# Identity transposes in the waits of the matmul engine, tied behind the last dense matmul

## The chip, the cores and the metric

The kernel runs on one core of a Trainium2 chip. The metric is the time of one execution of the whole program on the device, in microseconds (us), lower is better. The engines are TensorE (PE: matmuls, and transposes done as matmuls against an identity matrix), VectorE (DVE), ScalarE (ACT), GpSimd (POOL) and SyncE (SP), whose queue issues most weight loads.

## The reference

256 tokens of width 1024 go through one block of one architecture and then two layers of another, all in float32.

```python
def reference(x, ...):
    x = first_block(x, p, ...)     # retention + sliding-window attention, merged, w_out;
                                   # then a mixture of 32 experts (top 2), then a gated embedding
    return second_block(x, c_2, ctx_2, ...)

def second_block(x, c, ctx, ...):
    for i in range(DEPTH_2):       # 2 layers, over x and over a context of the same form
        mod = (s_c @ w_mod[i] + b_mod[i])[:, None, :]
        ...
        h = modulate(rms_norm_2(x, g_norm1[i]), sh1, sc1)
        p = h @ w_in[i]
        ...                        # neighbourhood attention, spatial gating, latent attention
        x_new = x + gt1 * mix
        x_new = x_new + gt2 * squared_relu_mlp(modulate(rms_norm_2(x_new, g_norm2[i]), sh2, sc2),
                                               ffn_w1[i], ffn_w2[i])
```

The change touches no value that reaches the output.

## The kernel before

Every weight is streamed from HBM once, in pieces of 128x1024 float32. Each dense product is done as three matmuls on split operands: ACT rounds a piece to its high part `wh` (L187), DVE subtracts to get the low part `wl` (L188), and PE accumulates high by high, high by low and low by high. `dense_b` (L268 to L270) keeps the activation stationary and streams up to 512 columns; `mm_a` (L245 to L247) keeps the weight stationary and streams the 256 tokens.

Between two dense products of the main path stands a norm: ACT sums the squares (L291, L299), DVE does a Newton iteration for the inverse root (`newton`, L178 to L183), ACT and DVE scale the rows (L321, L322), PE transposes them by 128x128 (`turn`, L332), DVE and ACT evacuate the result with gain and shift (L343) and split it (L187, L188). Only then can the next dense product begin.

Work that is off this path is run beside it: the context's layer beside the router and the experts of block 1 (`moe`), the modulation matrices (`w_mod`, L709, L720), the context's keys. A scheduler of the framework orders the instructions of each engine from the order and the priorities in which the program was traced, so a stage's place in the queue of an engine is set when the program is built; on the chip each engine then takes its queue strictly in order.

PSUM has four pairs of banks, `pd`, `cd` (dense results) and `ps`, `cs` (small results, such as transposes), taken in turn. Of the stages named below: `dense_b` in block 1's output projection (writes `pd`); `router`, whose transposes are L767 and whose products are L772; `experts`, whose gathered rows are transposed at L925 and multiplied by the expert weights at L935 (the weights lie in slots `ew`, loaded by SP as slots come free), beside the context's latent keys (L1472 to L1489, transposed in `heads_T`, L1444); `gm_mix`, whose transposes are L1581 and products L1592; and `ffn`, which calls `turn`. L1317 transposes queries, L1080 multiplies queries and keys.

Of the kernel before, what the change touches and what calls it, by code (L numbers as in the profile page):

```python
# [163 lines left out]
class Build:  # L164
    def __init__(self, nc, tc, ins, out, dbg=None):
        self.nc, self.tc, self.i, self.out, self.dbg = nc, tc, ins, out, dbg or {}
        self.sides = []
        self.made = 0
        self.W2, self.wturn = None, 0
        self.flip = 0  # L170
        self.sturn = 0

    def newton(self, st, ss, n, scale, eps=EPS, eng=None):
# [65 lines left out]
    def mm_a(self, ps, x, w, f):  # L239
        mm = self.nc.tensor.matmul  # L240
        xh, xl = x
        n = len(w)
        s = slice(f * 128, f * 128 + 128)
        for k, (wh, wl) in enumerate(w):
            mm(ps, wh[:, s], xh[:, k], start=k == 0, stop=False)  # L245
            mm(ps, wh[:, s], xl[:, k], start=False, stop=False)  # L246
            mm(ps, wl[:, s], xh[:, k], start=False, stop=k == n - 1)  # L247

# [7 lines left out]

    def dense_b(self, st, x, view, put, width=512):
        mm = self.nc.tensor.matmul
        xh, xl = x
        K = view.shape[1]  # L260
        for c in range(0, view.shape[2], width):
            ps = [st.dense()[:, :width] for _ in range(2)]
            for k0, w in self.pieces(st, view[:, :, c:c + width]):
                for t in range(2):
                    s = slice(t * 128, t * 128 + 128)
                    for j, (wh, wl) in enumerate(w):
                        k = k0 + j
                        mm(ps[t], xh[:, k, s], wh, start=k == 0, stop=False)  # L268
                        mm(ps[t], xh[:, k, s], wl, start=False, stop=False)  # L269
                        mm(ps[t], xl[:, k, s], wh, start=False, stop=k == K - 1)  # L270
            for t in range(2):
                put(t, c, ps[t])

    def evac(self, dst, src):
# [49 lines left out]

    def turn(self, st, xn, gain=None, mod=None, out=None):
        nc = self.nc
        h, l = out or self.hl(st, 8)
        for j in range(4):
            ps = st.small_ps().rearrange("p (k t) -> p k t", k=2)
            for kk in range(2):  # L330
                for t in range(2):
                    nc.tensor.transpose(ps[:, kk, t * 128:t * 128 + 128], xn[t][:, 2 * j + kk], self.ident)  # L332
            if mod is None:
                for kk in range(2):
                    k = 2 * j + kk
                    g = gain[:, k:k + 1]
                    nc.scalar.activation(h[:, k], ps[:, kk], AF.Copy, scale=g)
                    nc.vector.scalar_tensor_tensor(l[:, k], ps[:, kk], g, h[:, k].bitcast(F32), op0=ALU.mult, op1=ALU.subtract)
            else:
                src = st.a(2).rearrange("p (k t) -> p k t", k=2)  # L340
                for kk in range(2):
                    k = 2 * j + kk
                    nc.vector.tensor_scalar(src[:, kk], ps[:, kk], mod[0][:, k:k + 1], mod[1][:, k:k + 1],  # L343
                                            op0=ALU.mult, op1=ALU.add)
                self.split(h[:, 2 * j:2 * j + 2], l[:, 2 * j:2 * j + 2], src)
        return h, l
# [10 lines left out]
    def run_all(self):  # L357
        nc, tc, i = self.nc, self.tc, self.i
        with ExitStack() as ctx:
# [61 lines left out]
            x0.rows(st)  # L421
            x0.turn(st)
            x0.start()
# [229 lines left out]
    def block1_out(self, st, mh):  # L653
        nc, i = self.nc, self.i

        def put_out(t, c, ps):
            xs = self.x[:, t, c:c + 512]
            nc.vector.tensor_tensor(xs, ps, xs, op=ALU.add)

        self.dense_b(st, mh, kp(i["w_out"][0], 8), put_out)  # L660

# [68 lines left out]
    def router(self, st, act):  # L730
# [32 lines left out]
        for j in range(4):  # L763
            ps = st.small_ps().rearrange("p (k t) -> p k t", k=2)
            for kk in range(2):
# [140 lines left out]
    def experts(self, st):  # L906
# [11 lines left out]
        for g in range(8):  # L918
            he = hes.pop()
            heT = st.a(4, tag="heT", bufs=1).rearrange("p (k s) -> p k s", k=8)  # L920
            for j in range(2):
                ps = st.small_ps().rearrange("p (k s) -> p k s", k=4)
                for kk in range(4):
                    c = (4 * j + kk) * 128
                    nc.tensor.transpose(ps[:, kk], he[:, c:c + 128], self.ident)  # L925
                self.evac(heT[:, 4 * j:4 * j + 4], ps)
            if g < 7:
                hes.append(gather(g + 1))
            pg = st.small_ps()
            for u in range(2):  # L930
                for kh in range(2):
# [221 lines left out]
class Layer:  # L1153
# [84 lines left out]

    def turn(self, st):
        self.xT = self.b.turn(st, self.xn, mod=(self.A[:, 0], self.mc[:, 0]), out=self.b.xT_tiles())  # L1240

# [318 lines left out]
    def gm_mix(self):  # L1560
# [26 lines left out]
        for j in range(2):  # L1587
            ps = st.small_ps().rearrange("p (g n q) -> p g n q", g=2, n=2)
            for gg in range(2):
# [41 lines left out]
    def ffn(self, meanwhile=None):  # L1631
# [3 lines left out]
        if meanwhile:  # L1635
            meanwhile()
        xT = b.turn(st, xn, mod=(self.A[:, 1], self.mc[:, 3]))
        w1 = pk(i["ffn_w1_2"][l], 8)
# [49 lines left out]
```

## Time and profile before

| what | value |
|---|---|
| median of 3 runs | 1928.05 us (1917.57, 1928.05, 1931.88) |
| the profiled execution | 1929.36 us, span 1926.9 us |
| PE | 1795.2 us busy, 93% of the span, 12572 matmuls |
| DVE, ACT, POOL | 1245.0 us (65%), 906.9 us (47%), 215.4 us (11%) |
| mean granted clock of PE | 0.976 |
| HBM | 232 GB/s over the span |

The profile is of one execution. "Idle before" is the time an engine stood still ahead of an instruction, and what follows the arrow is the instruction whose end released it. The granted clock is the share of full speed that PE was given: 1.0 is 2.4 GHz and 0.5 is 1.2 GHz.

### The profile page before, as it was taken

To read this page: it belongs to the slowest core of one execution; us is meant where nothing else is said; L and a number is where in the kernel's file an instruction comes from. 1 tells how busy PE (TensorE), PEld (TensorE's weight loads), DVE (VectorE), ACT (ScalarE), POOL (GpSimd) and SP (SyncE) were. 2 spreads that over 40 slices of the span, in tenths; PEclk is the share of its full clock that TensorE was granted. 3 is DMA by queue.
4 is the path that set the end of the run, shared out by engine and by line. 5 is a ranking of instruction groups with operands and counts; after the bars stand their busy time and mean duration, and the time that the engine had idled before them with its cause. 6 is when DMAs were issued, how large, how long until landed. Compare 5 with 4: busy or idle time off the path is not lost. (4 is left out here: it accounts for less than half of the span.)

```text
span 1926.9 us, 32425 instructions
## 1 busy us (share of the span) xinstructions
PE 1795.2 (93%) x12572; PEld 1474.3 (77%) x12572; DVE 1245.0 (65%) x2377; ACT 906.9 (47%) x1395; POOL 215.4 (11%) x209
## 2 busy tenths in 40 slices
PE   5999877999999999979899989999999899998998
PEld 3677856677786777765676878799998888787998
DVE  3554566664566545454768597866678887866665
ACT  3433434473444433334534465544456555554443
POOL 3000110100110101110121010011100210010110
PEclk9999988999999999989999999999999999998999
DMA  9788856889999998977787752555667655254652
GB/s 283 240 314 281 270 158 223 283 292 335 346 330 373 312 356 320 350 271 265 239 252 211 225 192 88 175 165 187 196 186 235 182 133 164 77 197 132 196 190 95
DMA packets 277172, 448.82 MB, mean 233 GB/s; under 512 B 35582, under 2 KB 182380, under 8 KB 276568
## 3 DMA queue, kind: packets, MB, share of 16 engines
q1 hardware_dynamic: 266344, 417.30, 65.0%
q0 software_dynamic: 10672, 29.43, 5.2%
q8 instruction: 99, 1.62, 0.3%
q14 instruction: 57, 0.47, 0.1%
HBM read 430.77 MB, written 15.86 MB: 232 GB/s over the span
## 5 line engine op out<-in xcount | busy, mean ns | idle before, releaser
L188 DVE TENSOR_TENSOR wl<-raw,wh 128x1024 fp32r<-128x1024 f32 (+2 forms) x484 | 610.3, 1265 | 366.5 <-ACT wh L187 207.3
L187 ACT ACTIVATE wh<-raw 128x1024 fp32r<-128x1024 f32 (+2 forms) x484 | 504.6, 1045 | 571.9 <-PE pd L246 117.6
L247 PE MATMUL pd<-xT,wl 128*128 128x256 f32 x384 | 108.9, 283 | 5.6 <-DVE wl L188 5.6
L245 PE MATMUL pd<-xT,wh 128*128 128x256 f32 x384 | 108.5, 283 | 0.4 <-DVE b_a L279 0.4
L246 PE MATMUL pd<-xT,wh 128*128 128x256 f32 x384 | 108.9, 283 | 0.0
L245 PE MATMUL cd<-b_a,wh 128*128 128x256 f32 x328 | 92.2, 281 | 0.0
L246 PE MATMUL cd<-b_a,wh 128*128 128x256 f32 x328 | 92.1, 281 | 0.0
L247 PE MATMUL cd<-b_a,wl 128*128 128x256 f32 x328 | 91.6, 279 | 0.0
L935 PE MATMUL ps<-ew,m_heT 128*32 128x256 f32 x1024 | 76.3, 386 | 8.2 <-DMA ew<-in_w_exp_up_dram 6.8
L247 PE MATMUL pd<-e_a,wl 128*128 128x256 f32 x288 | 82.3, 286 | 0.4 <-DVE wl L188 0.4
L245 PE MATMUL pd<-e_a,wh 128*128 128x256 f32 x288 | 82.4, 286 | 0.0
L246 PE MATMUL pd<-e_a,wh 128*128 128x256 f32 x288 | 81.8, 284 | 0.0
L246 PE MATMUL cd<-xT,wh 128*128 128x256 f32 x288 | 81.6, 283 | 0.0
L247 PE MATMUL cd<-xT,wl 128*128 128x256 f32 x288 | 81.3, 282 | 0.1
L245 PE MATMUL cd<-xT,wh 128*128 128x256 f32 x288 | 81.3, 282 | 0.0
L247 PEld LDWEIGHTS pd<-xT,wl 128*128 128x128 f32 x384 | 72.4, 189 | 8.8 <-DVE wl L188 6.4
L245 PEld LDWEIGHTS pd<-xT,wh 128*128 128x128 f32 x384 | 72.2, 188 | 4.3 <-issue 3.1
L246 PEld LDWEIGHTS pd<-xT,wh 128*128 128x128 f32 x384 | 72.2, 188 | 2.8 <-issue 2.5
L268 PE MATMUL cd<-wh,xT 128*128 128x512 f32 (+2 forms) x208 | 73.0, 352 | 0.0
L269 PE MATMUL cd<-wl,xT 128*128 128x512 f32 (+2 forms) x208 | 72.4, 348 | 0.1
L270 PE MATMUL cd<-wh,xT 128*128 128x512 f32 (+2 forms) x208 | 72.3, 348 | 0.0
L1609 POOL TENSOR_TENSOR xres<-xres,b_a 128x512 f32<-128x512 f32 x24 | 37.5, 1561 | 307.0 <-DVE b_a L1607 307.0
(719 smaller groups left out, 5036.7 us busy)
## 6 DMA issues: line engine op xcount, KB each, us to landing
raw<-in_ffn_w_dram SPq DMA_DIRECT2D x192, 512.0 KB, 4.6
raw<-in_w_in_dram SPq DMA_DIRECT2D x168, 512.0 KB, 5.2
raw<-in_w_mod_dram SPq DMA_DIRECT2D x96, 512.0 KB, 5.7
ew<-in_w_exp_gate_dram SPq DMA_DIRECT2D x64, 512.0 KB, 7.5
ew<-in_w_exp_up_dram SPq DMA_DIRECT2D x64, 512.0 KB, 8.3
ew<-in_w_exp_down_dram SPq DMA_DIRECT2D x64, 512.0 KB, 7.2
raw<-in_w_out_dram SPq DMA_DIRECT2D x32, 512.0 KB, 5.8
raw<-in_w_in_dram SPq DMA_DIRECT2D x16, 504.0 KB, 3.6
```

What stands on the lines that cost most here:

```text
L187: self.nc.scalar.activation(h, src, AF.Copy)
L188: self.nc.vector.tensor_tensor(l, src, h.bitcast(F32), op=ALU.subtract)
L245: mm(ps, wh[:, s], xh[:, k], start=k == 0, stop=False)
L246: mm(ps, wh[:, s], xl[:, k], start=False, stop=False)
L247: mm(ps, wl[:, s], xh[:, k], start=False, stop=k == n - 1)
L268: mm(ps[t], xh[:, k, s], wh, start=k == 0, stop=False)
L269: mm(ps[t], xh[:, k, s], wl, start=False, stop=False)
L270: mm(ps[t], xl[:, k, s], wh, start=False, stop=k == K - 1)
L935: mm(pg[32 * e:32 * e + 32, u * 256:u * 256 + 256], heT[:, kh * 4 + k, 32 * e:32 * e + 32], ws[e][:, k], start=kh == 0 and k == 0, stop=kh ...
L1609: (nc.vector if stats else nc.gpsimd).tensor_tensor(xs, xs, tmp, op=ALU.add)
```

## The change

A new method `idle(ps, n)` issues n PE transposes of the identity matrix into a PSUM bank that the next real results overwrite. They are 128x128 float32, and nobody reads them. Each batch is traced under `issue_after(self.last)`: a program-order edge, without a semaphore, behind the last dense matmul traced so far by `mm_a` or `dense_b`. There are 270 in eight places: **B**, 14 ahead of block 1's output projection; **C**, 56 ahead of the router's transposes; **D**, 22 ahead of the first expert group's transposes and 36 ahead of its first products; **A**, 48 ahead of the transposes that begin the second block; **E**, 16 ahead of `gm_mix`'s products in each of the two layers of x; **F**, 22 and 40 ahead of the transposes of the two layers' `ffn`.

```diff
@@ class Build @@
+        self.last = None
...
@@ mm_a @@
-            mm(ps, wl[:, s], xh[:, k], start=False, stop=k == n - 1)
+            last = mm(ps, wl[:, s], xh[:, k], start=False, stop=k == n - 1)
+        self.last = last.ins
...
-    def dense_b(self, st, x, view, put, width=512):
+    def dense_b(self, st, x, view, put, width=512, wait=0):
...
             ps = [st.dense()[:, :width] for _ in range(2)]
+            if c == 0:
+                self.idle(ps[0], wait)
...
-                        mm(ps[t], xl[:, k, s], wh, start=False, stop=k == K - 1)
+                        last = mm(ps[t], xl[:, k, s], wh, start=False, stop=k == K - 1)
+                self.last = last.ins
...
+    def behind(self):
+        if self.last is not None and any(z is self.last for z in self.nc.cur_bb.bb.instructions):
+            return self.tc.issue_after(self.last)
+        return nullcontext()
+
+    def idle(self, ps, n):
+        with self.behind():
+            for _ in range(n):
+                self.nc.tensor.transpose(ps[:, :128], self.ident, self.ident)
...
-    def turn(self, st, xn, gain=None, mod=None, out=None):
+    def turn(self, st, xn, gain=None, mod=None, out=None, wait=0):
...
-            ps = st.small_ps().rearrange("p (k t) -> p k t", k=2)
+            ps = st.small_ps()
+            if j == 0:
+                self.idle(ps, wait)
+            ps = ps.rearrange("p (k t) -> p k t", k=2)
...
-            x0.turn(st)
+            x0.turn(st, 48)
...
-        self.dense_b(st, mh, kp(i["w_out"][0], 8), put_out)
+        self.dense_b(st, mh, kp(i["w_out"][0], 8), put_out, wait=14)
@@ router @@
+            if j == 0:
+                self.idle(ps, 56)
@@ experts @@
+                if g == j == 0:
+                    self.idle(ps, 22)
...
             pg = st.small_ps()
+            if g == 0:
+                self.idle(pg, 36)
@@ gm_mix @@
+            if j == 0 and self.mode == "x":
+                b.idle(ps, 16)
@@ ffn @@
-        xT = b.turn(st, xn, mod=(self.A[:, 1], self.mc[:, 3]))
+        xT = b.turn(st, xn, mod=(self.A[:, 1], self.mc[:, 3]), wait=(22, 40)[l] if self.mode == "x" else 0)
```

Since the scheduler orders all queues anew, the change moves more than it adds: besides the 270 transposes some 2300 of 12600 PE rows stand in another order, 300 of DVE, 170 of ACT and 70 of SP, in about 160 places on PE. Two activation-table loads of ACT fall away. Three places follow. Line numbers after the change are higher: L268 to L270 are L272 to L274 there, L245 to L247 are L246 to L248, L925 is L949, L935 is L961, L1444 is L1470, L1317 is L1343, L1581 is L1607, L1592 is L1621, L1080 is L1106, and `idle` is L287.

Place D on PE, before: the context's last projection (`xT`, not shown) has ended, and the first experts' rows (`m_he`, gathered by DMA) are transposed ahead of and between the products that make the context's latent keys (`c_a`).

```order
L1404 MATMUL cs<-ident,c_ck 128x128 x2
L925 MATMUL ps<-ident,m_he 128x128 x7
L268 MATMUL cd<-wh,c_a_2988 128x512
L269 MATMUL cd<-wl,c_a_2988 128x512
L268 MATMUL cd<-wh,c_a_2988 128x512
L269 MATMUL cd<-wl,c_a_2988 128x512
L925 MATMUL ps<-ident,m_he 128x128
L270 MATMUL cd<-wh,c_a_2989 128x512 x2
L935 MATMUL ps<-ew,m_heT 32x256 x5
L268 MATMUL cd<-wh,c_a_2988 128x512
```

The same place after. The name `c_a_3187` is the input of the context's latent queries, whose product is the last dense one traced ahead of the experts.

```order
L274 MATMUL cd<-wh,c_a_3188 128x384
L287 MATMUL ps<-ident 128x128 x22
L949 MATMUL ps<-ident,m_he 128x128 x8
L272 MATMUL cd<-wh,xT 128x512
L287 MATMUL ps<-ident 128x128 x30
L1470 MATMUL cs<-ident,c_a_3202 96x128 x2
L287 MATMUL ps<-ident 128x128
L1470 MATMUL cs<-ident,c_a_3202 96x128 x6
L287 MATMUL ps<-ident 128x128 x4
L1470 MATMUL cs<-ident,c_a_3202 96x128 x4
L287 MATMUL ps<-ident 128x128
L1470 MATMUL cs<-ident,c_a_3202 96x128 x4
```

The transposes L925 and the expert products L935 stood ahead of the latent keys, queries and their head transposes; now they stand behind both dense products.

Place E on PE, layer 1, before: the last product of the latent-query projection, the transposes of the neighbourhood queries (L1317), and then the layer's next projection (`pd<-xT`) runs on, 25 matmuls of it, with L1080 and L1581 among them, up to L1592 (the first rows of it).

```order
L268 MATMUL cd<-wh,xT 128x256
L269 MATMUL cd<-wl,xT 128x256
L270 MATMUL cd<-wh,xT 128x256
L1317 MATMUL cd<-ident,b_a_15167 128x128 x4
L245 MATMUL pd<-xT,wh 128x256
L246 MATMUL pd<-xT,wh 128x256
L247 MATMUL pd<-xT,wl 128x256
L245 MATMUL pd<-xT,wh 128x256
```

The same place after, up to the row ahead of L1592 (L1621 here).

```order
L287 MATMUL cs<-ident 128x128 x16
L1343 MATMUL cd<-ident,b_a_15381 128x128 x4
L246 MATMUL pd<-xT,wh 128x256
L247 MATMUL pd<-xT,wh 128x256
L248 MATMUL pd<-xT,wl 128x256
L246 MATMUL pd<-xT,wh 128x256
L247 MATMUL pd<-xT,wh 128x256
L1607 MATMUL ps<-ident,b_a_15733 128x128 x4
L1106 MATMUL cs<-b_a_14909,b_qh 128x512
L1106 MATMUL cd<-b_a_14909,b_qh 128x512
L248 MATMUL pd<-xT,wl 128x256
L246 MATMUL pd<-xT,wh 128x256
```

Of 25 matmuls of that projection seven are left between the query transposes and `gm_mix`; the other 18 stand behind L1592 now.

Place C on ACT, before: the sums of squares (`r_junk`, L291) of the router's norm stand behind the split of the context's weights (`wh`).

```order
L187 ACTIVATE wh<-raw 128x1008 x2
L187 ACTIVATE wh<-raw 128x672
L291 ACTIVATE r_junk,r_ss<-xres 128x1024
L1252 ACTIVATE c_a_2636<-cd 128x512
L291 ACTIVATE r_junk,r_ss<-xres 128x1024
L1252 ACTIVATE c_a_2636<-cd 128x512
```

The same place after, where L306 is the sum of squares and L188 the split.

```order
L188 ACTIVATE wh<-raw 128x1024 x3
L188 ACTIVATE wh<-raw 128x1008
L306 ACTIVATE r_junk,r_ss<-xres 128x1024 x2
L188 ACTIVATE wh<-raw 128x1008
L1278 ACTIVATE c_a_2706<-cd 128x512
L188 ACTIVATE wh<-raw 128x672
L1278 ACTIVATE c_a_2706<-cd 128x512
```

Both sums of squares now stand two splits earlier in ACT's queue.

## Rows read from the trace of the kernel before

**Rows 1.** The page's busy time, and the granted clock in 40 slices.

```profile
PE 1795.2 (93%) x12572; PEld 1474.3 (77%) x12572; DVE 1245.0 (65%) x2377; ACT 906.9 (47%) x1395; POOL 215.4 (11%) x209
...
PEclk9999988999999999989999999999999999998999
```

**Rows 2.** Windows: us, busy of PE, PEld, DVE, ACT, POOL, clock, DMA, GB/s.

```profile
228.80:235.50 6.70, 5.35 (x13) 3.67 (x12) 4.00 (x5) 2.46 (x3) 3.74 (x3) 0.50 0.75 213
273.20:283.30 10.10, 4.99 (x15) 2.72 (x16) 5.98 (x11) 0.60 (x1) 1.07 (x2) 0.50 0.28 112
314.10:320.90 6.80, 5.21 (x22) 3.69 (x23) 1.37 (x3) 1.66 (x4) 0.96 (x1) 0.50 0.50 164
331.20:337.90 6.70, 5.14 (x15) 2.21 (x16) 0.20 (x1) 1.32 (x2) 0.00 (x0) 0.50 1.04 421
924.40:928.40 4.00, 3.78 (x16) 3.14 (x16) 2.18 (x5) 1.70 (x3) 0.00 (x0) 0.50 0.93 166
928.60:932.00 3.40, 3.40 (x19) 2.13 (x14) 3.13 (x7) 1.45 (x3) 0.00 (x0) 1.00 0.43 122
1249.40:1256.10 6.70, 5.87 (x28) 5.91 (x29) 5.88 (x12) 2.53 (x4) 0.00 (x0) 0.50 0.28 78
1529.30:1532.60 3.30, 2.87 (x13) 2.86 (x14) 2.28 (x7) 0.36 (x1) 0.00 (x0) 0.50 0.43 113
1737.50:1747.60 10.10, 6.21 (x27) 5.44 (x28) 6.80 (x17) 4.21 (x5) 0.00 (x0) 0.50 0.01 5
348.00:640.00 292.00, 287.21 (x2320) 219.83 (x2313) 176.47 (x329) 137.12 (x230) 25.63 (x28) 1.00 0.92 327
690.00:840.00 150.00, 135.52 (x1023) 104.23 (x1022) 71.24 (x78) 53.47 (x64) 18.50 (x15) 0.97 0.92 338
```

**Rows 3.** Timeline of PE, stage A: start, duration, operation, idle before.

```profile
924.49 0.45 PE L332 MATMUL ps<-ident,b_a 128*128 128x128 f32 x1 [6.55 <-issue]
...
926.61 1.06 PE L332 MATMUL ps<-ident,b_a 128*128 128x128 f32 x4
...
927.47 1.06 PE L332 MATMUL cs<-ident,b_a 128*128 128x128 f32 x4
```

**Rows 4.** Timeline of PE, stage B.

```profile
226.92 0.50 PE L268 MATMUL pd<-wh,e_a 128*128 128x512 f32 x1 [3.24 <-ACT e_tg L669]
...
231.72 0.80 PE L268 MATMUL pd<-wh,e_a 128*128 128x512 f32 x1 [1.35 <-DVE e_tg L675]
```

**Rows 5.** Timeline of ACT, DVE and PE, stage C.

```profile
269.88 1.04 ACT L291 ACTIVATE r_junk<-xres 128x1024 bf16<-128x1024 f32 x1
...
274.74 4.03 DVE L760 SCALAR_TENSOR_TENSOR c_a<-xres,r_ny,c_a 128x1024 f32<-128x1024 f32 x2
...
277.00 0.66 PE L767 MATMUL ps<-ident,c_a 128*128 128x128 f32 x2 [7.82 <-issue]
```

**Rows 6.** Timeline of PE and DVE, stage D.

```profile
315.69 1.72 PE L925 MATMUL ps<-ident,m_he 128*128 128x128 f32 x7 [3.80 <-DMA m_he<-xnscr,ints]
...
322.75 0.40 PE L270 MATMUL cd<-wh,c_a 128*128 128x512 f32 x1
...
331.64 1.06 PE L935 MATMUL ps<-ew,m_heT 128*32 128x256 f32 x2 [5.34 <-DMA ew<-in_w_exp_up_dram]
...
330.45 0.42 DVE L1489 TENSOR_TENSOR c_a<-c_krr,c_ny 128x256 f32<-128x256 f32 x1
```

**Rows 7.** Timeline of PE and DVE, stage E, layer 1.

```profile
1529.73 2.16 PE L1592 MATMUL cs<-b_a,b_a 128*128 128x128 f32 x8 [3.61 <-ACT b_a L277]
...
1523.34 5.64 DVE L1575 TENSOR_TENSOR b_a<-b_a,b_a 128x512 f32<-128x512 f32 x2
```

**Rows 8.** Timeline of PE, stage F, layer 0 and then layer 1.

```profile
1245.03 1.03 PE L332 MATMUL cs<-ident,b_a 128*128 128x128 f32 x8
...
1250.23 1.09 PE L332 MATMUL cs<-ident,b_a 128*128 128x128 f32 x4 [4.16 <-DVE b_a L343]
...
1741.53 1.54 PE L332 MATMUL cs<-ident,b_a 128*128 128x128 f32 x6 [2.32 <-ACT b_a L322]
```

More of the change, by code (lines that the diff above doesn't have):

```diff
@@ L1 @@
-from contextlib import ExitStack
+from contextlib import ExitStack, nullcontext
 import numpy as np
@@ L763, in router @@
         for j in range(4):
-            ps = st.small_ps().rearrange("p (k t) -> p k t", k=2)
+            ps = st.small_ps()
+            if j == 0:
+                self.idle(ps, 56)
+            ps = ps.rearrange("p (k t) -> p k t", k=2)
             for kk in range(2):
@@ L921, in experts @@
             for j in range(2):
-                ps = st.small_ps().rearrange("p (k s) -> p k s", k=4)
+                ps = st.small_ps()
+                if g == j == 0:
+                    self.idle(ps, 22)
+                ps = ps.rearrange("p (k s) -> p k s", k=4)
                 for kk in range(4):
@@ L1237, in rows, with turn @@
         self.xn = b.norm_rows(st, self.x, stats=self.mode == "x")
-    def turn(self, st):
-        self.xT = self.b.turn(st, self.xn, mod=(self.A[:, 0], self.mc[:, 0]), out=self.b.xT_tiles())
+    def turn(self, st, wait=0):
+        self.xT = self.b.turn(st, self.xn, mod=(self.A[:, 0], self.mc[:, 0]), out=self.b.xT_tiles(), wait=wait)
     def head_stats(self, ps, wd, hd, dst):
@@ L1587, in gm_mix @@
         for j in range(2):
-            ps = st.small_ps().rearrange("p (g n q) -> p g n q", g=2, n=2)
+            ps = st.small_ps()
+            if j == 0 and self.mode == "x":
+                b.idle(ps, 16)
+            ps = ps.rearrange("p (g n q) -> p g n q", g=2, n=2)
             for gg in range(2):
```

## The prediction

> **What bounds the kernel now.** I read the busy time and the granted clock of the page first, then a table of windows over the stretches in which the clock was at half, then the timeline of each of the eight places.
>
> PE is busy for 93% of the span, and its clock drops by a notch in a few of the 40 slices [rows 1]. So PE sets the time, in two ways: by the work it has, and by the clock it is granted. Seven stretches of the second group ran at 0.50 (1.2 GHz) and lie at places that the change touches: B at 228.8 us, C at 273.2, D at 314.1 and 331.2, F at 1249.4 and 1737.5, E at 1529.3. An eighth, A, is shown from 924.4 on [rows 2]. Each comes with a wait of PE: 3.24 us at B [rows 4], 7.82 at C [rows 5], 3.80 and 5.34 at D [rows 6], 3.61 at E in layer 1 [rows 7], 4.16 at F in layer 0 and, in layer 1, 2.32 behind an earlier one [rows 8], 6.55 at A [rows 3]. So there are two things to win: not the waits, whose ends are set by ACT, DVE or a DMA, but the half clock behind them.
>
> The ceiling follows from the busy time of PE in these stretches, since work done at 0.5 takes twice its time: 5.35 + 4.99 + 5.21 + 5.14 + 3.78 + 5.87 + 2.87 + 6.21 = 39.4 us [rows 2], half of which is 19.7 us, or 1.02% of the execution. More than that can't come from the clock at these places.
>
> **What one added transpose costs.** Eight take 1.03 us at full clock, the last one's latency included [rows 8]; four at half clock begin 0.86 us apart (926.61 and 927.47) [rows 3]. I take 0.11 us at full clock and 0.21 at half: 270 of them are 30 us, if none lay in a wait.
>
> Do transposes of this kind hold or raise the clock? Between 924.40 and 928.40 PE did sixteen matmuls, all of them L332, the same 128x128 float32 transposes, at 0.50; from 928.60 on the clock is 1.00 [rows 2, 3]. No dense product ran in between. So in this trace transposes alone stood ahead of a rise, and I take it that they also keep the clock up.
> The Trainium skill says otherwise on the page "TensorE: Matmul & The Clock Gate", section "Part 4: PE-mode transpose": the full clock does not engage for transposes, because they do not count as busy in the same way. This trace disagrees, with its 0.50 ahead of 928.40 and 1.00 from 928.60; the page's rule speaks against the whole change and is the second rival below.
>
> **The places, one by one** (minus is a gain).
>
> B, 14 transposes, 1.5 us. They write the bank that ends the wait of 3.24 us, so they stand behind the same ACT instruction (L669) and can't fill it; they run from 226.92 on, beside a weight split that PE waits for anyway, and ahead of the wait of 1.35 us [rows 4]. That keeps PE at work just before 228.8, where the clock falls. Of 5.35 us at half clock [rows 2] those behind 231.72 are PE-bound, about 3.6 us, half of which is 1.8. Taken: −1.8, between 0 and −2.7.
>
> C, 56 transposes, 6.1 us. They are tied behind the dense product traced last, and the order puts them ahead of the context's next product, 48 matmuls that ended in front of the wait. So that product slides into the wait by 6.1 us and leaves about 2 of its 7.82 us [rows 5]; the cover is real work. What sets the wait's end is the chain from the sums of squares (269.88), over the Newton steps, to L760, two of them in 4.03 us from 274.74 on [rows 5]. The sums of squares stood behind splits that wait for that product's matmuls; they are moved ahead of two of them, so the chain is late by some 0.3 us and not by 6. Half of the 4.99 us done at 0.50 is 2.5 [rows 2]. Taken: −2.0; if the chain is late after all, +6.
>
> D, 58 transposes. Here the order changes most. Before, the first experts' transposes and products ran while DVE worked on the latent keys: 7.9 us from the end of the last key product (322.75 and 0.23) to the end of L1489 (330.87) [rows 6]. Now all of the experts' work stands behind the dense product of the latent queries, and PE has nothing to do in these 7.9 us. A second chain of the same form, for the queries, follows their product; it is filled by 22 and 30 added transposes and by 8 useful ones of 0.9 us. So 15.8 us hold 0.9 of useful work, where before the waits were 3.80 and 5.34 [rows 6]. Against that, one fall of the clock takes the place of two, which saves 2.6 of the 5.2 us that both cost (half of 5.21 and 5.14) [rows 2]. Sum: 15.8 − 0.9 − 9.1 − 2.6 = +3.2. Taken: +3, between −5 (no fall, the waits as before) and +9 (the added transposes at half clock on top, 58 × 0.1).
>
> A, 48 transposes, 5.2 us. They lie in the wait of 6.55 us ahead of 924.49 [rows 3] with room to spare and hold the clock. DVE evacuates and splits what PE turns, and that sets the end. Taken: −0.6, between 0 and −1.9 (half of 3.78) [rows 2].
>
> F. In layer 0, 22 transposes (2.4 us) stand ahead of the eight at 1245.03, whose result is used only after the wait of 4.16 us [rows 8]; they fit. Half of 5.87 us is 2.9, and the splits of DVE (5.88 us of 6.70 busy) [rows 2] keep part of it: −1.7. In layer 1, 40 of them (4.3 us) fill most of the first wait, but the wait of 2.32 us ahead of 1741.53 comes behind two transposes [rows 8] and stays empty, so the clock may fall once more, for less time. Of half of 6.21 us I take half: −1.5, between 0 and −3.1.
>
> E. In layer 1 what ends the wait is not PE's to hasten: DVE's L1575, two of them in 5.64 us [rows 7], and the evacuation queued behind it. DVE's order is the same there. But the products that filled the time ahead of it are moved behind it: 18 matmuls at 0.12 us (2320 in 287 us [rows 2]) are 2.2 us of work that has to be done later, in exchange for 16 transposes that do nothing. The wait grows from 3.6 to some 5 us, and the clock falls as before. In layer 0, where the clock did not fall, 16 transposes cost 1.8 us at most in themselves and as many products are deferred; some land in later waits. Taken together: +2.5, between −1.4 (half of 2.87) and +6.
>
> The other moved rows of PE, DVE and ACT, chiefly in the experts' stage, I take at nothing: from 348 to 640 us PE is busy for 287 of 292 us [rows 2], whatever the order. If that cover is gone, it is the last rival.
>
> **The sum.** −1.8 − 2.0 + 3 − 0.6 − 1.7 − 1.5 + 2.5 = −2.1. The profiled execution took 1929.36 us and lies 1.3 above the median of the three runs. So 1929.4 − 2.1 − 1.3 = 1926.0 us, a change of 0.1%.
>
> **The rivals.**
> First, the full gain: every one of these stretches stays at full clock, and what is moved falls into other waits. That is the ceiling of 19.7 us: 1929.4 − 19.7 − 1.3 = 1908. For it speaks that six places of eight have the added work in or right ahead of the wait; against it, the empty waits at D, E and F.
>
> Second, transposes do not hold the clock. Then A, B, C and F give nothing, D costs 3 + 2.6 for the fall that stays and about 1.5 more where the added transposes at half clock outlast their chain, and E costs 2.5: +9.6, so 1937. The rise at 928.6 speaks against it [rows 2].
> By that rule of the Trainium skill this would be the outcome; the trace speaks against it by the 1.00 of that row.
>
> Third, slower than before: the experts' late start. L935 frees the slots into which SP loads expert weights, and its first products already stood ahead of 331.64, where the next waited for an `ew` load [rows 6]. Moved behind two dense products and two chains they begin some 20 us later. From 348 to 640 us the DMA engines are busy for 0.92 of the time, so 23 us of slack would take that up just about; from 690 to 840, at 0.92 again, PE already stands still for 14.5 of 150 us [rows 2]. If the loads can't be caught up, PE waits there for all 20 us: 1929.4 + 20 − 1.3 = 1948. It decides once the transfers of that stage need more than 0.93 of their time.
>
> **Chances.** The sum 0.57, the full gain 0.18, no hold on the clock 0.12, late experts 0.13. A measurement of this kernel can tell about 1% from no change (here 1908.8 to 1947.3), so faster by over 1% has 0.18, within 1% 0.69, slower 0.13. The range is from 1907, just below the ceiling, to 1940, above the second rival and the upper ends at D and E; it leaves out the third.
>
> **What would show it.** Right: the clock at 1.00 behind A, B, C and F in layer 0; a wait of some 8 us at D with the clock at 0.50 behind it, and the first L935 near 343 us; L1592 in layer 1 still behind a wait of 4 to 5 us. Wrong: the clock at 0.50 behind A or C although PE was busy with transposes up to then; no wait at D; or longer waits of L935 for `ew` loads between 690 and 840 us.

## The result, and the profile after

The changed kernel took 1936.78 us (median of 7 runs, 1932.07 to 1941.62) against 1926.35 us for the kernel before run beside it: a ratio of 1.0051, 95% interval 1.0026 to 1.0076. It is slower by 10 us, where a gain of 2 us was forecast. The time lies within the stated range, but the sign is wrong.

The page of the profile after, PE's busy time and its clock in 40 slices, against [rows 1]:

```profile
PE 1822.9 (94%) x12842; PEld 1504.7 (78%) x12842; DVE 1242.7 (64%) x2377; ACT 902.4 (47%) x1393; POOL 214.3 (11%) x209
...
PEclk8999989999999999999999999999999999999999
```

PE is busy for 27.7 us more (1822.9 against 1795.2), nearly the 30 us that 270 transposes were priced at. The clock looks better, its mean 0.977 against 0.976 in the profiles. So the added work was done, and much of it did not lie where PE had nothing to do.

The windows of the profile after at the eight places, in the columns of [rows 2]:

```profile
225.10:231.70 6.60, 6.45 (x45) 5.74 (x46) 6.15 (x10) 4.62 (x5) 0.75 (x1) 1.00 0.78 239
274.00:284.10 10.10, 7.18 (x22) 3.90 (x23) 4.37 (x5) 0.60 (x1) 1.07 (x2) 0.50 0.44 144
316.70:321.70 5.00, 0.00 (x0) 0.00 (x0) 4.41 (x19) 2.38 (x6) 0.56 (x1) 1.00 0.79 249
321.80:328.50 6.70, 4.02 (x16) 2.74 (x16) 3.68 (x18) 2.00 (x3) 0.00 (x0) 0.50 0.14 51
916.50:925.60 9.10, 8.60 (x76) 7.08 (x72) 7.36 (x43) 5.34 (x8) 0.00 (x0) 1.00 0.91 236
1249.40:1256.90 7.50, 5.74 (x43) 5.01 (x42) 4.31 (x9) 5.76 (x8) 0.00 (x0) 1.00 0.44 137
1257.00:1260.40 3.40, 3.40 (x18) 3.40 (x17) 3.40 (x7) 1.65 (x3) 0.00 (x0) 0.50 0.17 67
1533.50:1540.20 6.70, 5.61 (x22) 5.21 (x23) 4.99 (x12) 1.11 (x2) 0.28 (x1) 0.50 0.34 113
1742.70:1747.00 4.30, 4.30 (x40) 4.12 (x38) 4.13 (x20) 2.40 (x5) 0.00 (x0) 1.00 0.53 189
1752.00:1755.30 3.30, 2.76 (x14) 2.39 (x13) 3.05 (x7) 1.26 (x2) 0.00 (x0) 0.50 0.00 0
348.00:640.00 292.00, 282.75 (x2333) 216.63 (x2333) 164.87 (x306) 126.59 (x217) 24.43 (x27) 0.99 0.93 334
690.00:840.00 150.00, 140.06 (x1073) 108.22 (x1071) 70.38 (x79) 53.65 (x64) 19.57 (x16) 1.00 0.96 352
```

B (225.1) and A (916.5) now run at 1.00, where [rows 2] had 0.50. At F the first wait of each layer does (1249.4, 1742.7), but the clock falls behind it all the same, for 3.4 us in each layer (1257.0, 1752.0), where it was at 0.50 for 7 and 10 us before. C (274.0) is at 0.50 for as long as before, 10 us; two other profiles with C's transposes (e2 and e5 below) have 6.8 us. At D there is a stretch from 316.7 in which PE does nothing at all, and half clock behind it. E (1533.5) is at 0.50 for 6.7 us, twice as long as before; but a second profile of the kernel before (e1) has 6.8 us there too. The waits that stand there now, in the timeline of PE after:

```profile
275.07 0.66 PE L788 MATMUL ps<-ident,c_a 128*128 128x128 f32 x2 [3.18 <-issue]
...
324.07 0.66 PE L1470 MATMUL cs<-ident,c_a 128*96 128x128 f32 x2 [7.39 <-DVE c_a L1515]
...
336.34 2.56 PE L287 MATMUL ps<-ident 128*128 128x128 f32 x22
...
340.07 3.49 PE L287 MATMUL ps<-ident 128*128 128x128 f32 x30
...
1534.59 2.16 PE L1621 MATMUL cs<-b_a,b_a 128*128 128x128 f32 x8 [4.09 <-ACT b_a L292]
...
1256.11 0.63 PE L350 MATMUL cs<-ident,b_a 128*128 128x128 f32 x4 [1.76 <-DVE b_a L361]
...
1751.59 1.26 PE L350 MATMUL cs<-ident,b_a 128*128 128x128 f32 x6 [2.57 <-ACT b_a L337]
```

C's wait has shrunk from 7.82 to 3.18 us [rows 5], but L767 (L788 here) is not earlier, and the clock still falls. At D the wait of 7.39 us for the latent keys is the one that was forecast; 52 transposes in two batches stand behind the query product, and the experts behind them. At E the wait ahead of L1592 (L1621) has grown from 3.61 to 4.09 us [rows 7]. F's first waits are filled, 1.76 us left of 4.16, and the wait of 2.57 us ahead of 1751.59 is there as forecast [rows 8].

To see where the time went, each matmul of one trace was paired with the same matmul of another (the n-th of its line, tiles and shape), and the median shift was taken at the ends of each stretch. The table gives the growth of this shift against the profile of before, in us; minus is a gain. The first column is a second profile of the same program as before (e1), so it tells how far one execution differs from another.

| stretch, us | same program (e1) | after | A, B, F (e3) | + C (e5) | + D (e6) | + D with 1 and 1 (e10) | without E (e2) | E alone (e4) |
|---|---|---|---|---|---|---|---|---|
| 205 to 246 (B) | -1.3 | -7.4 | -7.8 | -8.2 | -7.4 | -7.3 | -8.2 | -1.0 |
| 246 to 300 (C) | 0.4 | 3.2 | 0.7 | 3.0 | -0.3 | -0.4 | 2.7 | -0.1 |
| 300 to 700 (D) | -0.1 | 8.3 | -3.0 | -3.4 | 11.0 | -1.8 | 8.2 | 0.4 |
| 700 to 865 | -5.0 | -5.6 | -4.5 | -4.4 | -4.6 | -3.4 | -4.5 | -0.3 |
| 865 to 1000 (A) | 5.8 | -5.1 | -5.4 | -0.4 | 0.6 | -4.4 | -4.1 | 2.9 |
| 1000 to 1145 (E, layer 0) | 5.3 | 9.0 | 4.2 | 3.1 | 3.6 | 7.8 | 4.9 | 4.4 |
| 1145 to 1280 (F, layer 0) | -0.7 | -1.3 | -2.4 | -2.4 | -2.4 | -0.6 | -2.5 | -0.5 |
| 1500 to 1640 (E, layer 1) | 2.7 | 5.1 | 2.0 | 2.0 | 1.9 | 2.8 | 1.9 | 2.8 |
| 1640 to 1765 (F, layer 1) | 0.3 | -1.4 | -0.1 | -0.4 | -0.1 | -0.2 | -0.2 | 0.0 |

Between 205 and 700 us the two profiles of one program agree within 1.5 us. From 700 on they differ by up to 6 us in a stretch, so single differences there are weak evidence, and the times below decide.

What differs between executions of one program goes largely with the granted clock. From 1000 to 1145 us e1 lost 5.3 us, and its clock was at 0.50 for 13.7 us there, where before's never fell:

```profile
1000.00:1145.00 145.00, 133.61 (x1063) 111.83 (x1062) 111.19 (x279) 70.47 (x127) 19.19 (x20) 1.00 0.66 204
...
1000.00:1145.00 145.00, 133.61 (x1030) 113.11 (x1029) 104.64 (x273) 67.42 (x123) 15.72 (x15) 0.95 0.65 199
```

The first line is before's, the second e1's. The times show the same: of 102 executions of the kernel before (one of 3497.6 us left out), the 32 with the lowest mean clock (0.972 on average) took 1932.6 us, and the 27 with the highest (0.977) 1923.9 us. So a growth in the table counts for the order of the queues only where the clock was the same in both profiles.

### The profile page after: what moved, and what is told of

The parts are those of the page before. It is cut to its first block, busy times and chain, and to the rows that moved or that the text cites. A ratio compares the mean times of both kernels' runs of the same rounds, so it can differ in the third digit from the quotient of the medians.

```text
span 1935.5 us, 32961 instructions
## 1 busy us (share of the span) xinstructions
PE 1822.9 (94%) x12842; PEld 1504.7 (78%) x12842; DVE 1242.7 (64%) x2377; ACT 902.4 (47%) x1393; POOL 214.3 (11%) x209
## 5 line engine op out<-in xcount | busy, mean ns | idle before, releaser
L188 ACT ACTIVATE wh<-raw 128x1024 fp32r<-128x1024 f32 (+2 forms) x484 | 504.8, 1045 | 590.4 <-PE cd L247 119.4
L248 PE MATMUL pd<-xT,wl 128*128 128x256 f32 x384 | 111.0, 289 | 4.3 <-DVE wl L189 4.3
L246 PE MATMUL pd<-xT,wh 128*128 128x256 f32 x384 | 110.3, 287 | 0.0
L247 PE MATMUL pd<-xT,wh 128*128 128x256 f32 x384 | 110.2, 287 | 0.0
L246 PE MATMUL cd<-b_a,wh 128*128 128x256 f32 x328 | 91.7, 280 | 0.0
L247 PE MATMUL cd<-b_a,wh 128*128 128x256 f32 x328 | 91.7, 280 | 0.0
L248 PE MATMUL cd<-b_a,wl 128*128 128x256 f32 x328 | 91.5, 279 | 0.0
L248 PE MATMUL cd<-xT,wl 128*128 128x256 f32 x288 | 82.2, 285 | 4.6 <-DVE wl L189 4.4
L248 PE MATMUL pd<-e_a,wl 128*128 128x256 f32 x288 | 83.1, 289 | 0.7 <-DVE wl L189 0.7
L246 PE MATMUL cd<-xT,wh 128*128 128x256 f32 x288 | 82.8, 287 | 0.0
L246 PE MATMUL pd<-e_a,wh 128*128 128x256 f32 x288 | 82.7, 287 | 0.0
L247 PE MATMUL pd<-e_a,wh 128*128 128x256 f32 x288 | 82.4, 286 | 0.0
L247 PE MATMUL cd<-xT,wh 128*128 128x256 f32 x288 | 81.6, 283 | 0.0
L248 PEld LDWEIGHTS pd<-xT,wl 128*128 128x128 f32 x384 | 74.5, 194 | 8.6 <-DVE wl L189 4.7
L246 PEld LDWEIGHTS pd<-xT,wh 128*128 128x128 f32 x384 | 74.3, 193 | 2.4 <-issue 1.9
L247 PEld LDWEIGHTS pd<-xT,wh 128*128 128x128 f32 x384 | 74.4, 194 | 1.4 <-issue 1.0
L272 PE MATMUL cd<-wh,xT 128*128 128x512 f32 (+2 forms) x208 | 73.7, 355 | 0.0
L961 PE MATMUL ps<-ew,m_heT 128*32 128x256 f32 x1024 | 72.5, 384 | 0.8 <-DMA ew<-in_w_exp_up_dram 0.6
L274 PE MATMUL cd<-wh,xT 128*128 128x512 f32 (+2 forms) x208 | 72.5, 349 | 0.0
```

The lines of the kernel that those rows point to most:

```text
L188: self.nc.scalar.activation(h, src, AF.Copy)
L248: last = mm(ps, wl[:, s], xh[:, k], start=False, stop=k == n - 1)
L274: last = mm(ps[t], xl[:, k, s], wh, start=False, stop=k == K - 1)
L961: mm(pg[32 * e:32 * e + 32, u * 256:u * 256 + 256], heT[:, kh * 4 + k, 32 * e:32 * e + 32], ws[e][:, k], start=kh == 0 and k == 0, stop=kh ...
```

## The experiments

All times are medians beside runs of the kernel before on the same chip; the ratio is to these, with its 95% interval. The diffs are against the changed kernel, that of e13 against the kernel of e1.

| kernel | time, us | ratio | interval |
|---|---|---|---|
| the changed kernel | 1936.8 | 1.0051 | 1.0026 to 1.0076 |
| e2, without E | 1932.7 | 1.0029 | 1.0010 to 1.0048 |
| e3 and e9, A, B and F | 1910.2, 1914.3 | 0.9915, 0.9923 | 0.9882 to 0.9948, 0.9901 to 0.9945 |
| e4, E alone | 1930.5 | 1.0021 | 1.0002 to 1.0041 |
| e5, A, B, F and C | 1921.7 | 0.9966 | 0.9940 to 0.9992 |
| e6, A, B, F and D | 1932.3 | 1.0026 | 1.0003 to 1.0050 |
| e7, A alone | 1923.6 | 0.9971 | 0.9948 to 0.9994 |
| e8, B alone | 1919.3 | 0.9954 | 0.9935 to 0.9973 |
| e10, A, B, F and D with 1 and 1 | 1917.8 | 0.9932 | 0.9909 to 0.9954 |
| e11, F alone | 1926.1 | 0.9986 | 0.9965 to 1.0006 |
| e12, B with one transpose | 1928.6 | 0.9993 | 0.9973 to 1.0013 |
| e13, the moved load, no transposes | 1924.9 | 0.9976 | 0.9952 to 1.0001 |
| e14, A, B, F and 16 at C | 1913.5 | 0.9930 | 0.9903 to 0.9956 |
| e15, A, F and the moved load | 1918.7 | 0.9951 | 0.9932 to 0.9971 |

**e1, all counts zero.** The order of every queue is that of the kernel before.

```diff
-        self.dense_b(st, mh, kp(i["w_out"][0], 8), put_out, wait=14)
+        self.dense_b(st, mh, kp(i["w_out"][0], 8), put_out, wait=0)
...
```

> All eight counts are zero, so the order of every queue is that of the kernel before: a second profile of the same program. If the 3.8 us that the changed kernel loses in the first 100 us, where nothing was changed, are variation between executions, this profile too differs from that of before by 1 to 5 us in that stretch, and stays within 1 us from there to the end. If they belong to the change, it follows the profile of before within 1 us throughout.

Its one execution took 1938.4 us, a time that the kernel before itself reaches in its slowest runs (up to 1938.5 beside e5 to e8). This profile is ahead of before's by 4 us at 250 us and by 9 us at 865 us, and loses ground from there on, in several stretches where no queue differs. The first reading holds: the 3.8 us that the changed kernel lost in the first 100 us are not the change's. Its second half does not: the profiles differ by more than 1 us later too, and by 9.6 us at the end.

**e2, without E; e3, A, B and F alone; e4, E alone.**

```diff
-                b.idle(ps, 16)
+                b.idle(ps, 0)
```

> The changed kernel without the transposes at E. Theory (useful products displaced at E are the largest loss): the changed kernel lost 7.6 us between 1000 and 1130 us and 5.2 us between 1510 and 1640 us; both go away, and the time is about 1924 us, 12.8 us below the changed kernel's 1936.8 and a little under the kernel before. Rival (the order between 1000 and 1130 us is spoilt by the transposes at A, which move the same stretch): only the 5.2 us of layer 1 go away, about 1931.5 us.

> Transposes at A, B and F alone. Theory: these are the places where the clock was won: 7.4 us at B, about 4 at A, 2.4 at F, so 13 to 14 us under the kernel before, about 1913 us. Rival (A's reordering costs 7.6 us after 1000 us): 6 us under it, about 1920 us.

> Transposes at E alone, 16 in each layer. Theory: E costs 12.8 us on its own, so about 1939 us. Rival (the stretch after 1000 us is A's): 5.2 us, about 1931.5 us. If E costs only what its 32 transposes take, 3.5 us, 1930 us.

Without E the time falls by 0.22% (1.0051 to 1.0029), some 4 us, which lies within the uncertainty of the two ratios; E alone adds 0.21%, 4 us as well, and that interval just leaves out 1. The theory of 12.8 us falls: of what it read from a single pair of traces between 1000 and 1145 us most is the clock, which was at 0.50 for 13.7 us there, as it was in e1, where nothing was changed. E costs about 4 us, near the 3.5 us that its 32 transposes take, which was the third reading; but e4's trace has 4.4 us between 1000 and 1145 us at a clock of 1.00, where more groups of L709 (the modulation matrices, see A below) stand in pieces than before. A, B and F alone come out as the theory had it, 0.85% under the kernel before. So the large loss must be C's and D's: without E it is all that is left between e2 and e3, 1.1%.

**e5 and e6, C and D each added to A, B and F; e7 and e8, A and B each alone.**

> A, B and F with the 56 transposes at C added. In the traces so far the stretch from 250 to 290 us lost 3.2 us in the changed kernel and 2.7 us without E, and 0.7 us without C. Theory (C costs: the router's chain of norm and scaling ends later, the wait is still over 3 us and the clock still falls): 2 to 3 us over the kernel with A, B and F, about 1912.5 us. Rival (C gains as predicted): 2 us under it, about 1908 us.

> A, B and F with the 58 transposes at D added. Theory (D is the largest loss, through what it moves: two chains of norms are exposed and the experts begin later): 11 to 20 us over the kernel with A, B and F, 1921 to 1930 us, with most of it lost between 310 and 560 us. Rival (the loss of the changed kernel against A, B and F is E's and C's): 3 us as predicted, 1913 us.

> A alone. Theory (the gain at A comes from the order: modulation matmuls that stood singly between dense products stand together, in fours, and some move into the wait): 4 to 6 us under the kernel before, 1921 to 1922 us, with 3 us of it won ahead of the added transposes, between 890 and 915 us. Rival (the gain is the clock's): 1 to 2 us, all of it behind them.

> B alone. Theory (the gain at B comes from a moved load: the context's rows are fetched one weight load earlier, so ACT does not stand behind them with the weight splits queued after): 6 to 7 us under the kernel before by 250 us, so about 1920 us, and no wait of PE of 3 us there. Rival (the gain is the clock's): 1.8 us, with the wait of 3.2 us still there.

D costs most: 1.1% of the time, and 14 us between 300 and 700 us (11.0 against -3.0). C costs too, 0.4 to 0.5% in the times and 2.3 us in its stretch (3.0 against 0.7); in e5's profile A's stretch is 5 us worse than in e3's as well, which is not explained. A gives 0.29%, B 0.46%.

At A the timeline of PE before shows what was to be won besides the clock (L709, the modulation matrices, eight matmuls on four groups of 32 columns of the array):

```profile
907.81 1.04 PE L709 MATMUL pd<-raw,sT 128*32 128x512 f32 x2
...
909.45 1.05 PE L709 MATMUL pd<-raw,sT 128*32 128x512 f32 x2
...
916.88 1.06 PE L709 MATMUL pd<-raw,sT 128*32 128x512 f32 x8
```

Two of them take as long as eight, 1.04 and 1.06 us, where they stand singly between dense products. The same place after (L709 is L727):

```profile
915.47 1.06 PE L727 MATMUL pd<-raw,sT 128*32 128x512 f32 x8
...
916.47 3.49 PE L287 MATMUL ps<-ident 128*128 128x128 f32 x30
...
919.89 1.07 PE L727 MATMUL pd<-raw,sT 128*32 128x512 f32 x8
...
920.89 2.18 PE L287 MATMUL ps<-ident 128*128 128x128 f32 x18
```

One group of eight that stood in four pairs now stands together, 1.06 us and not 4 times 1.04, and a group of eight lies inside the wait, between the added transposes. That is 4 us of order: all ten profiles with A's transposes gain 4.5 us here ahead of the first batch, and none of the others does. So far the theory holds. But the same new order moves another group ahead and breaks it into four pairs. The same eight matmuls before, and then with A alone (e7):

```profile
1057.34 1.07 PE L709 MATMUL pd<-raw,sT 128*32 128x512 f32 x8
```

```profile
1027.94 1.04 PE L727 MATMUL pd<-raw,sT 128*32 128x512 f32 x2
...
1029.23 1.04 PE L727 MATMUL pd<-raw,sT 128*32 128x512 f32 x2
...
1030.52 1.05 PE L727 MATMUL pd<-raw,sT 128*32 128x512 f32 x2
...
1031.82 1.05 PE L727 MATMUL pd<-raw,sT 128*32 128x512 f32 x2
```

Between 1000 and 1145 us e3, e7 and e9 lose 3.4 to 4.2 us, although their clock is at 1.00 throughout; e8 and e13, with the old order here and the same clock, lose none. So the order gives back nearly all that it won. What is left to explain A's 0.29% is the clock: in the seven profiles without A's transposes it was at 0.50 for 6.8 to 13.7 us around this place, with PE at work for 3.4 to 9.8 us of that, and in none of the ten with them. No run has A's order without its transposes, so the two shares of the time are not measured apart.

At B ACT tells it. Before, and then with B alone (L291 is L306, L669 is L687):

```profile
222.16 1.06 ACT L291 ACTIVATE e_junk<-e_a 128x1024 bf16<-128x1024 f32 x1 [5.98 <-DMA e_a<-in_ctx_dram]
...
226.29 0.57 ACT L669 ACTIVATE e_tg<-pd 128x512 f32<-128x512 f32 x1
```

```profile
214.37 1.06 ACT L306 ACTIVATE e_junk<-e_a 128x1024 bf16<-128x1024 f32 x1 [0.81 <-DMA e_a<-in_ctx_dram]
...
221.46 0.58 ACT L687 ACTIVATE e_tg<-pd 128x512 f32<-128x512 f32 x1
```

Before, ACT stood for 5.98 us until the context's rows arrived, with L669 and two weight splits queued behind; PE's wait of 3.24 us [rows 4] ended with L669. With B the load stands one weight load earlier in SP's queue, ACT waits 0.81 us, and PE has no wait of 1 us there.

**e9, A, B and F again; e10, D with one transpose in each batch; e11, F alone; e12, B with one.**

```diff
-                    self.idle(ps, 22)
+                    self.idle(ps, 1)
...
-                self.idle(pg, 36)
+                self.idle(pg, 1)
```

> The kernel with A, B and F a second time, beside the next three on one chip. Theory (it is the fastest here): 0.7 to 1.0% under the kernel before. Rival (the 0.85% of its first six runs were luck): within 0.4% of it, the sum of A alone and B alone being 0.75%.

> A, B and F with D's two batches cut from 22 and 36 transposes to one each. The two that are left still stand behind the last dense product and still hold back all of the experts behind it. Theory (D's loss lies in the order, two chains exposed and the experts late): the loss against A, B and F between 300 and 700 us, 14 us with all of D's transposes, stays over 8 us, and the time is above 1920 us. Rival (the loss is the transposes' own time, 6 us at full clock and up to 12 at half): less than 3 us of it is left, about 1912 us.

> F alone. Here no other row moves on any engine, so this is the clock by itself: 22 transposes in one wait of 4.2 us and 40 in one of 5.9 us. Theory (transposes hold the clock where they fill the wait): 1.0 stays granted in layer 0 around 1250 us and 1.8 us are won there, 0 to 0.3 in layer 1, where a second wait of 2.3 to 2.6 us follows; 0.1% in all, within the noise of the time. Rival (transposes do not hold it): the clock is at 0.50 behind both waits as before, and nothing is won.

> B with one transpose in place of 14: the order of every queue is that of the kernel before, without the context's rows moved up. Theory (B's gain of 0.46% is the moved load): no change against the kernel before, and PE's wait of 3 us at 224 us and ACT's of 6 us for the context's rows are back. Rival (the transpose itself does it): faster by 0.3% or more.

A, B and F repeat, 0.77% under the kernel before. e10 decides against my theory: with two transposes in place of 58, and the experts tied back as before, nearly the whole loss is gone (0.9932 against 0.9923 without D, and 1.0026 with all of D). The stretch from 300 to 700 us loses 1.2 us, not 14. What the 58 do is seen in PE's timeline, e6 first:

```profile
315.42 0.66 PE L1470 MATMUL cs<-ident,c_a 128*96 128x128 f32 x2 [7.39 <-DVE c_a L1515]
...
329.02 2.56 PE L287 MATMUL ps<-ident 128*128 128x128 f32 x22
...
332.76 3.50 PE L287 MATMUL ps<-ident 128*128 128x128 f32 x30
...
337.14 0.42 PE L1470 MATMUL cs<-ident,c_a 128*96 128x128 f32 x2 [0.88 <-DVE c_a L1452]
...
341.54 1.93 PE L961 MATMUL ps<-ew,m_heT 128*32 128x256 f32 x30
```

And e10, with one transpose each:

```profile
314.90 0.66 PE L1470 MATMUL cs<-ident,c_a 128*96 128x128 f32 x2 [7.39 <-DVE c_a L1515]
...
328.60 1.04 PE L949 MATMUL ps<-ident,m_he 128*128 128x128 f32 x8
...
330.58 1.93 PE L961 MATMUL ps<-ew,m_heT 128*32 128x256 f32 x32
...
336.48 0.42 PE L1470 MATMUL cs<-ident,c_a 128*96 128x128 f32 x2
...
340.71 1.93 PE L961 MATMUL ps<-ew,m_heT 128*32 128x256 f32 x32
```

Both have the wait of 7.39 us. Behind the query product e10 does 32 of the experts' products (L961) from 330.58 on and dense products of the context, all ahead of the head transposes at 336.48. In e6 the wait for the same heads is filled with 22 and 30 transposes, and these products come behind it, from 339.93 on. The transposes did not fill an empty wait; they took the place of work that would have filled it. Their own time is 6.4 us at 0.11 each; the stretch loses 13 against e10. By 450 us 10 of the 13 are lost. The 6 or so beyond their own time are not traced one by one; the orders of e6 and e10 differ in several hundred rows of PE, and from 513 to 516 us e6 has a fall of the clock that e10 has not.

e11 gives 0.14%, within its uncertainty. Its windows in layer 0:

```profile
1237.00:1246.20 9.20, 7.42 (x51) 6.43 (x50) 6.01 (x11) 7.02 (x9) 0.00 (x0) 1.00 0.50 156
1246.30:1249.70 3.40, 3.40 (x18) 3.40 (x17) 3.30 (x8) 1.58 (x3) 0.00 (x0) 0.50 0.08 31
1249.80:1256.00 6.20, 6.20 (x54) 6.04 (x54) 2.54 (x3) 1.94 (x2) 0.00 (x0) 1.00 0.01 3
```

The clock still fell, for 3.4 us, behind a wait of 1.78 us that the 22 transposes left. In e1 and e12, with nothing in that wait, the stretch gains 0.7 to 1.1 us against before's profile, here 1.3, and 2.4 in the kernels with A, B and F where it did not fall. So that transposes help at F is not shown by F alone. All profiles together speak for it in layer 0: the clock fell at this place in all seven without F's transposes, and in three (after, e10, e11) of the ten with them, though each of the ten has a wait of about 1.8 us left. In layer 1 it is at 0.50 for 10.2 us without them and for 3.4 to 6.9 with them, and the stretch hardly gains (1640 to 1765 us in the table). e12 is as expected: without the changed order B gives nothing, and ACT waits again:

```profile
219.23 1.06 ACT L306 ACTIVATE e_junk<-e_a 128x1024 bf16<-128x1024 f32 x1 [5.06 <-DMA e_a<-in_ctx_dram]
```

**e13, the load moved and no transposes; e14, 16 at C; e15, A, F and the load.**

```diff
-        self.nc.sync.dma_start(self.x, src)
+        with self.b.tc.high_priority(offset=20): self.nc.sync.dma_start(self.x, src)
```

> The kernel before with no transposes at all: the load of the context's rows is given a higher priority, which moves it ahead of one weight load in SP's queue, and one weight split behind the context's sums of squares on ACT; nothing moves on PE. Theory (B's gain is this load): 0.4 to 0.5% under the kernel before, the wait of 3 us at 224 us gone. Rival (B's transposes are needed to hold the clock at 228 us): the wait shrinks and about 0.25%, with the 1.8 us of the clock missing.

> A, B and F with 16 transposes at C in place of 56. Theory (C's loss is that 56 transposes hold the context's next product back by 6 us, and with it the weight splits behind which the sums of squares stand on ACT): 16 hold it back by 1.7 us, inside the wait of 7.8 us, and the time stays within 0.2% of A, B and F. Rival (any transposes in that place cost, through the place alone): 0.3% or more over A, B and F.

> The moved load of e13 with A and F, without B's, C's, D's and E's transposes. Theory (the gains add up): 0.29 by A, 0.14 by F, 0.45 by the load, 0.8 to 0.9% under the kernel before, like A, B and F. Rival (B's 14 transposes give something of their own): 0.2% or more behind A, B and F.

The load alone gives 0.24% (0.9976, its interval ends at 1.0001), the number of the rival, though not for its reason, as the clock held; its stretch gains 5.6 of the 8.2 us that B gives there, where kernels without B gain about 1. ACT's wait in e13 is still 3.43 us, and in e15, with the same moved load, 1.71:

```profile
219.59 1.06 ACT L306 ACTIVATE e_junk<-e_a 128x1024 bf16<-128x1024 f32 x1 [3.43 <-DMA e_a<-in_ctx_dram]
```

```profile
214.00 1.06 ACT L306 ACTIVATE e_junk<-e_a 128x1024 bf16<-128x1024 f32 x1 [1.71 <-DMA e_a<-in_ctx_dram]
```

So the moved load is most of B's gain in the trace, some 4.6 of 7.2 us in e13; in e15, also without B's transposes, the stretch gains 7.3 us, as much as in several kernels with them (7.3 to 8.2). The load stands at the same place of SP's queue in e8, e13 and e15, and what differs is how long it took from issue to ACT's start: 8.1, 10.7 and 9.0 us. Whether B's 14 transposes add anything was not told apart from this spread. In e13 the clock did not fall at 228 us although PE waited there for 1.75 us, so the transposes were not needed to hold it. e15 is 0.3% behind A, B and F, as its rival had it, but the intervals of the ratios overlap. e14 is as expected: 16 transposes at C cost nothing that can be measured (0.9930 against 0.9915 and 0.9923); it takes the 56 to lose.

## Why the prediction was wrong

**The mechanism that was forecast for the clock is there, where the wait was really filled.** At A the clock stays at 1.00. (So it does at B, but in e13 without a transpose: there the wait itself went, with the moved load.) At A the stretch from 916.5 to 925.6 has the 48 added transposes, the 16 of real data and one group of L709, and no dense product, at 1.00.
So the rule of the Trainium skill that was weighed ("TensorE: Matmul & The Clock Gate", section "Part 4: PE-mode transpose", by which the full clock does not engage for transposes) does not agree with these runs either: 9.1 us of such work at 1.00 in the profile after. The rival built on it (1937; its own terms add up to 1937.7) came within 1 us of the time, and that is luck: the reason was another.

The places where the clock was to win were forecast at −7.6 us together. In the seven runs of the changed kernel the mean clock was 0.980 against 0.975 for the kernel before, by which at most 9 us less were lost to the half clock (an estimate: 0.005 of 1930 us). So the clock gave about what was expected, and the failure lies in what the added work and the new order cost: up to some 20 us, not the 5.5 of D and E.

**D, taken at +3, is the step that failed most.** Its sum was right on the first chain: the wait of 7.4 us stands there (7.9 forecast), with one fall of the clock behind it. It was wrong on the second: "it is filled by 22 and 30 added transposes" took the wait for the queries as empty otherwise. In e10 it is filled by the experts' products and the context's dense ones. D's loss is 14 us in the trace and 1.1% in the time.

**C, taken at −2.0, came out at +2 to +3 us in the trace.** The chain was to be late by 0.3 us. In ACT's timeline after, the sums of squares (L306) do stand ahead of two splits, but the two splits ahead of them wait for the matmuls of the product that 56 transposes held back:

```profile
263.54 1.06 ACT L188 ACTIVATE wh<-raw 128x1024 fp32r<-128x1024 f32 x1 [7.82 <-PE cd L274]
...
266.34 1.05 ACT L188 ACTIVATE wh<-raw 128x1008 fp32r<-128x1008 f32 x1 [1.74 <-PE cd L274]
...
267.29 1.04 ACT L306 ACTIVATE r_junk<-xres 128x1024 bf16<-128x1024 f32 x1
...
269.51 1.03 ACT L188 ACTIVATE wh<-raw 128x1008 fp32r<-128x1008 f32 x1
```

ACT stands for 7.82 us until 263.54, and the sums of squares begin at 267.29. Counted from the end of block 1's last product, they begin 11.9 us after it in e3 (256.85 against 244.99) and 12.8 us in e5 with C (261.13 against 248.37); the router's first transpose follows 19.0 us after it in e3 (263.95) and 20.6 us in e5 (268.92), so the chain is 1.6 us late. The wait that is left, 3.18 us, was taken at 2, and the clock falls behind it, for 10.2 us as before (6.8 in e2 and e5). The 6 us named for a late chain were too much, the 0.3 too little; the sign turned on it.

**A, taken at −0.6, and B, at −1.8, were too small.** They give 0.46% (B) and 0.29% (A), 14 us together, more than the whole ceiling for the clock at these two places (2.7 and 1.9 us). At B the step that failed is that "the other moved rows" were taken at nothing: one load of SP ahead of one other gives most of the gain. At A the moved rows win 4.5 us and lose nearly as much again by 1145 us. What was mis-sized there is the ceiling: it was read from 924.4 us on in one profile, in which half of PE's work at 0.50 was 1.9 us; the other six profiles without A's transposes give 1.7 to 4.9 us.

**E, taken at +2.5, cost about 4 us** by two pairs of times, of which one alone is clear of noise. The wait ahead of L1592 grew as forecast, though by less: it is 4.1 us in both profiles with E's transposes and 3.2 to 3.7 in all fifteen without. **F, taken at −3.2,** is 0.14% or 2.7 us in the times, not told from zero (−6.8 to +1.2 us by the interval); in the traces it is up to 2.4 us in layer 0, where the clock did not fall, and about nothing in layer 1.

**The third rival, late experts, did not come.** The first L935 stands at 347.2 us (343 was named), yet from 348 to 640 us the DMA share is 0.93, and from 690 to 840 PE does 140.1 us of work against 135.5 before [rows 2].

In the times: A, B and F together −0.8%, E +0.2%, D +1.1% and C +0.4 to 0.5% on top of A, B and F when added singly. The sum of these is about +1.0%, and the changed kernel has +0.5%; C and D together (e2 against e3) cost 1.1% and not 1.5%. Each ratio is uncertain by 0.2 to 0.35%, so these sums do not clearly disagree, and whether the places act on each other is left open.

The version that the experiments point to is the change without C, D and E: 0.8% under the kernel before, twice measured.

## What to carry to other kernels

Filler placed on an engine that a scheduler orders is not only its own time: it is a weight on the order of everything, so compare the built queues, and price a moved DMA and a broken-up group before the clock. Follow such a move to the end of the program: A's order joined one group of matmuls and broke another. Put filler only where the built order has no useful work that could stand there, and test each place alone; here three places win 0.8% and three lose more. Ahead of a wait, first ask what the releasing engine is itself waiting for: a load that is issued one place earlier removed most of what 14 transposes were meant to cover. And before a gain or loss in a trace is put down to the order, compare the granted clock of the two stretches.

## What the runs showed of the hardware

Eight matmuls on four groups of 32 columns of the array took 1.06 us standing together, and two of them 1.04 us, so a pair between dense products costs as much as the whole group. Two executions of one program differed by up to 6 us within stretches of 150 us, with no row of any queue different, and largely where the granted clock differed (at 0.50 for 13.7 us in one and never in the other, from 1000 to 1145 us). The clock was held at 1.00 through 9.1 us of transposes and small matmuls, yet fell behind a wait of 1.78 us at F (e11) and not behind one of 1.75 us at B (e13), nor behind the same wait of 1.8 us at F in seven other profiles.
